# A two-layer hybrid decoder on one core: half-size products in the fourth feed-forward, weight sums on VectorE and by DMA, and memory by stages

## The chip, the core and the metric

The kernel runs on one core of a Trainium2 chip. A core has a matrix engine (TensorE, PE in the rows; its weight loads are listed as PEld), three engines for elementwise work (VectorE or DVE, ScalarE or ACT, GpSimd or POOL), a queue engine (SyncE or SP) and 16 DMA engines that all queues share. The metric is the time of one execution in microseconds (us), lower is better. The time before is the median of three runs.

## The reference, cut to what matters

A sequence of 512 rows with 1024 features goes through two layers. Each layer is a feed-forward, a mixer and a feed-forward. Layer 0 mixes by attention, layer 1 by a state-space scan (S5). So there are four feed-forwards, and the fourth is the last thing computed.

```python
def rmsnorm(x, g):
    xf = x.astype(jnp.float32)
    y = xf * lax.rsqrt(jnp.mean(xf * xf, axis=-1, keepdims=True) + NORM_EPS)
    return (y * g.astype(jnp.float32)).astype(x.dtype)

def swiglu(h, w_gate, w_up, w_down):            # 1024 -> 2816 -> 1024
    return (jax.nn.silu(h @ w_gate) * (h @ w_up)) @ w_down

for i in range(2):
    x = x + 0.5 * swiglu(rmsnorm(x, ffn1_norm[i]), ffn1_gate[i], ffn1_up[i], ffn1_down[i])
    h = rmsnorm(x, mix_norm[i])
    x = x + (diff_fox_mixer(h, ...) if i % 2 == 0 else s5_mixer(h, ...))
    x = x + 0.5 * swiglu(rmsnorm(x, ffn2_norm[i]), ffn2_gate[i], ffn2_up[i], ffn2_down[i])
```

## The kernel before

x lies in on-chip memory, transposed, as 8 tiles of 128 features by 512 rows. Every number that goes into a large product is split into a rounded high part and the rest (`wh` and `wl` for weights, `xh` and `xl` for the normed x, `ah` and `al` for activations), and mm3 (L135) makes a product from three matmuls: high by high, high by low, low by high. Each matmul loads its own 128x128 weight block.

Weights come through the class Stream (L24). A unit is a load on SyncE's queue into one of 4 buffers `raw` of 2048 columns (8 KB in each partition, 1024 KB in all for gate and up). A group is half a unit: ScalarE casts it to `wh` (L77), VectorE subtracts to get `wl` (L79, or L318 and L323 where the subtraction is put off). `ahead` (L101) splits three groups ahead of TensorE and loads three units beyond them.

A feed-forward (ffn, L261) follows ffn_order: 22 tiles of 128 inner features, each one gate and one up product of 8 x 3 matmuls of 512 columns (tile `ps_gu`), and after 6, 12, 17 and 22 tiles a down pass of 8 output blocks (`ps_d`, 6 or 5 tiles each). post (L268) multiplies by the inverse root R, applies silu and splits the activation; upd (L314) adds the block to x. The norm's square sums are collected by norm_sum, stats1 (L221) sums them over partitions on TensorE and takes the root on VectorE in 13 short operations, stats2 (L229) spreads it. In the last down pass the callback `nxt` (in build, L1500) runs for every x block: in feed-forward three it is s5_in (L1215), which copies x into another order (`xp`), stores it to DRAM (dU) and reloads it rearranged (`U`).

Order of the instructions is that of the program text on every engine (`manual_schedule`). Work that fills gaps is written as generators in the list k.bg: attn_setup and s5_tables run beside feed-forward one, s5_ops (L1115) and s5_frames beside two and three. tick (L172) advances them after each gate or up product by 1.4 us of counted VectorE time in feed-forwards two and three (L302) and after each down block but the last pass's by 0.6 of that (L345); a yield of "wait" ends the call early. drain (L183) runs what is left to its end; it stands after feed-forwards one (L1548) and three (L1553).

s5_ops makes the weights of the scan. For each of 4 units it has 4 blocks j: three VectorE operations make `e`, four small matmuls (L1175, tile `ps_s`) follow, then VectorE scales the results, and `dW` and `dY` are stored. At the end of a unit the kernel vector `kq` is stored to DRAM (dK), read back by eight DMAs into `tr`, copied by ScalarE in 16 pieces to `to` (L1209) and stored as `dT`. The scan (s5, L1259) waits for the U tiles, loads dW, dT and dY as `raw`, and uses rotation tables `F5` that s5_frame loads from DRAM, 1 MB for each of four; tables 0 and 1 in the background, 2 and 3 at the first block of the last down pass.

Of the kernel before, what the change touches and what calls it, by code (L numbers as in the profile page):

```python
# [17 lines left out]
GROUPS = [(0, 6), (6, 6), (12, 5), (17, 5)]  # L18
# [5 lines left out]
class Stream:  # L24
# [3 lines left out]
    RAW = 4  # L28

    def __init__(self, nc, raw, hl, ahead_load=3, ahead_split=3):  # L30
        self.nc, self.raw, self.hl = nc, raw, hl
        self.AL, self.AS = ahead_load, ahead_split
        self.units, self.gr = [], []
        self.nl = self.ns = self.cur = self.done = 0
        self.rt, self.wt = {}, {}

    def add(self, ap, ncols, grs, split=True):
        u = len(self.units)
        self.units.append((ap, ncols))
        for a, b in grs:  # L40
            self.gr.append((u, a, b, split))

    def load(self, pieces=((0, 2048),)):
        ap, n = self.units[self.nl]
        t = self.raw.tile([P, 2048], F32, tag="raw", name="raw")
        self.rt[self.nl] = t
        self.nl += 1
        for a, b in pieces:
            self.nc.sync.dma_start(t[:, a:min(b, n)], ap[:, a:min(b, n)])
            yield  # L50

    def load_to(self, u, force=False):
        while self.nl <= min(u, len(self.units) - 1):
            if not force and self.nl - self.RAW >= self.done:
                break
            for _ in self.load():
                pass

    def split_to(self, g, pieces=None, later=None):
        while self.ns <= min(g, len(self.gr) - 1):  # L60
            u, a, b, sp = self.gr[self.ns]
            self.load_to(u, True)
            r = self.rt[u]
            if sp == "pairs":
                h = self.hl.tile([P, 1024], F32R, tag="wh", name="wh")
                z = h[:, :2 * (b - a)].rearrange("p (k two c) -> p k two c", two=2, c=8)
                v = r[:, a:b].rearrange("p (k c) -> p k c", c=8)
                self.nc.scalar.copy(z[:, :, 0], v)
                self.nc.vector.tensor_tensor(z[:, :, 1], v, z[:, :, 0].bitcast(F32), ALU.subtract)
                self.wt[self.ns] = (h, None)  # L70
                self.done = u + 1
            elif sp:
                h = self.hl.tile([P, 1024], F32R, tag="wh", name="wh")
                lo = self.hl.tile([P, 1024], F32R, tag="wl", name="wl")
                for c0, c1 in pieces or ((0, b - a),):
                    rest = (lo[:, c0:c1], r[:, a + c0:a + c1], h[:, c0:c1].bitcast(F32), ALU.subtract)
                    self.nc.scalar.copy(h[:, c0:c1], r[:, a + c0:a + c1])  # L77
                    if later is None:
                        self.nc.vector.tensor_tensor(*rest)  # L79
                    else:  # L80
                        later.append(rest)
                self.wt[self.ns] = (h, lo)
                if self.ns + 1 == len(self.gr) or self.gr[self.ns + 1][0] != u:
                    self.done = u + 1
            else:
                self.wt[self.ns] = (r[:, a:b], None)
            self.ns += 1

    def next(self):
        g = self.cur  # L90
        self.cur += 1
        if g and not self.gr[g - 1][3]:
            self.done = self.gr[g - 1][0] + 1
# [3 lines left out]
    def finish(self):  # L97

        self.done = self.gr[self.cur - 1][0] + 1

    def ahead(self, later=None):  # L101

        g = self.cur
        if g < len(self.gr):
            e = min(g + self.AS, len(self.gr) - 1)
            while not self.gr[e][3] and e > g:
                e -= 1
# [1547 lines left out]
```

## Time and profile before

| | us |
|---|---|
| median of 3 runs | 1898.06 |
| lowest, highest | 1897.71, 1898.67 |
| the profiled execution | 1897.74 |
| its span, first to last instruction | 1895.7 |
| TensorE busy in it | 1881.8 |
| VectorE, ScalarE, GpSimd busy | 1127.4, 671.3, 100.8 |

The four feed-forwards take most of the span: gate, up and down products run from 5 to 376, from 645 to 1383 and from 1531 to 1892 us; attention lies in the first gap, the S5 scan and its gated product in the second. A row of a timeline gives start, duration, engine, line and operation, with the idle time before it and what ended it in square brackets. A row of a group gives the count, the busy time and the mean of one in ns. A row of a table of windows gives the length, then for each engine the busy time and its count of instructions, then the granted clock of TensorE, the busy share of the DMA engines and GB/s.

### The profile page before, as it was taken

Reading aid. Unit: us, or ns where it says so; the run is one execution under the profiler, and the core shown is the slowest. Engines: PE = TensorE matmul, PEld = TensorE weight load, DVE = VectorE, ACT = ScalarE, POOL = GpSimd, SP = SyncE. Lnnn points to the kernel's source line nnn. Section 1 sums busy time; section 2 is a strip of 40 time slices with the busy share of each in tenths; the row PEclk is TensorE's granted clock in tenths of the full one; section 3 lists DMA queues with packets and bytes.
Section 4 is the critical chain, followed back from the end, with each engine's and each line's share of the span. In section 5 each row is a group of like instructions: output and inputs, shape, how many; then the busy total and the mean of one; then the engine's idle time right before and its main releaser. Section 6 shows DMA issues by size and latency. Waiting matters only on the chain.

```text
span 1895.7 us, 22606 instructions
## 1 busy us (share of the span) xinstructions
PE 1881.8 (99%) x8738; PEld 1557.1 (82%) x8740; DVE 1127.4 (59%) x2153; ACT 671.3 (35%) x1104; POOL 100.8 (5%) x184
## 2 busy tenths in 40 slices
PE   8999999999999999999999999999999999999999
PEld 6888888877788888888888888888888888888887
DVE  6787676657685665456557556444484654444443
ACT  5222222434557432322324332322363432222221
POOL 1000111000001000100100100100000000000000
PEclk9999999999999999999999999999999999999999
DMA  6333334234132323423523442433476322323221
GB/s 250 106 106 101 129 107 137 90 111 128 53 85 52 126 80 132 161 100 106 177 102 119 143 145 95 161 128 109 155 247 234 134 86 92 106 84 106 73 100 45
DMA packets 62812, 227.40 MB, mean 120 GB/s; under 512 B 23776, under 2 KB 23904, under 8 KB 46704
## 3 DMA queue, kind: packets, MB, share of 16 engines
q1 hardware_dynamic: 42736, 192.47, 29.7%
q0 software_dynamic: 11504, 31.36, 5.4%
q10 hardware_dynamic: 8464, 2.12, 0.5%
q8 instruction: 69, 1.13, 0.3%
q14 instruction: 39, 0.32, 0.1%
HBM read 196.17 MB, written 26.61 MB: 118 GB/s over the span
## 4 chain that ended last, share of the span: by engine, by line
PE 96%; DVE 1%; ACT 1%; DMA 1%; issue 1%; SPq 0%; DVEq 0%; ACTq 0%
PE ps_gu L137 17%; PE ps_gu L138 17%; PE ps_gu L139 17%; PE ps_d L137 8%; PE ps_d L139 8%; PE ps_d L138 8%; PE ps_p L423 2%; PE ps_p L425 2%; PE ps_p L424 2%; PE ps_g L137 2%; PE ps_g L138 2%; PE ps_g L139 2%; PE ps_s L1175 1%; PE ps_w L137 1%; PE ps_w L138 1%; PE ps_w L139 1%
## 5 line engine op out<-in xcount | busy, mean ns | idle before, releaser
L137 PE MATMUL ps_gu<-xh,wh 128*128 128x512 f32 x1408 | 552.1, 392 | 4.5 <-ACT xh L195 4.3
L138 PE MATMUL ps_gu<-xl,wh 128*128 128x512 f32 x1408 | 548.7, 390 | 0.3 <-DVE xl L196 0.3
L139 PE MATMUL ps_gu<-xh,wl 128*128 128x512 f32 x1408 | 548.8, 390 | 0.0
L77 ACT CAST wh<-raw 128x1024 fp32r<-128x1024 f32 (+3 forms) x354 | 333.9, 947 | 496.9 <-PE ps_d L138 237.3
L79 DVE TENSOR_TENSOR wl<-raw,wh 128x1024 fp32r<-128x1024 f32 (+3 forms) x235 | 260.2, 1110 | 163.9 <-ACT wh L77 162.1
L137 PEld LDWEIGHTS ps_gu<-xh,wh 128*128 128x128 f32 x1408 | 264.6, 188 | 60.6 <-ACT xh L195 4.6
L139 PEld LDWEIGHTS ps_gu<-xh,wl 128*128 128x128 f32 x1408 | 264.6, 188 | 55.7
L138 PEld LDWEIGHTS ps_gu<-xl,wh 128*128 128x128 f32 x1408 | 264.8, 188 | 55.2 <-DVE xl L196 1.2
L137 PE MATMUL ps_d<-ah,wh 128*128 128x512 f32 x704 | 274.9, 391 | 0.0
L139 PE MATMUL ps_d<-ah,wl 128*128 128x512 f32 x704 | 274.0, 389 | 0.0
L138 PE MATMUL ps_d<-al,wh 128*128 128x512 f32 x704 | 273.9, 389 | 0.0
L315 DVE SCALAR_TENSOR_TENSOR x<-ps_d,x 128x512 f32<-128x512 f32 x128 | 88.5, 692 | 183.1 <-PE ps_d L139 182.9
L274 DVE TENSOR_TENSOR u<-ps_gu,R 128x512 f32<-128x512 f32 x88 | 60.8, 691 | 180.7 <-PE ps_gu L139 180.7
L139 PEld LDWEIGHTS ps_d<-ah,wl 128*128 128x128 f32 x704 | 132.2, 188 | 27.7
L138 PEld LDWEIGHTS ps_d<-al,wh 128*128 128x128 f32 x704 | 132.2, 188 | 27.2
L137 PEld LDWEIGHTS ps_d<-ah,wh 128*128 128x128 f32 x704 | 132.2, 188 | 27.1
L277 ACT CAST ah<-u 128x512 fp32r<-128x512 f32 x88 | 54.7, 621 | 253.7 <-DVE u L275 251.3
L272 ACT ACTIVATE g<-g 128x512 f32<-128x512 f32 x88 | 55.6, 632 | 208.2 <-DVE g L271 208.2
L318 DVE TENSOR_TENSOR wl<-raw,wh 128x1024 fp32r<-128x1024 f32 (+2 forms) x101 | 104.8, 1038 | 0.3 <-ACT wh L77 0.3
L279 DVE TENSOR_TENSOR al<-u,ah 128x512 fp32r<-128x512 f32 x88 | 60.9, 692 | 60.5 <-ACT ah L277 60.5
L423 PE MATMUL ps_p<-wh,xh 128*128 128x512 f32 x192 | 78.0, 406 | 0.0
L425 PE MATMUL ps_p<-wh,xl 128*128 128x512 f32 x192 | 75.1, 391 | 0.0
(299 smaller groups left out, 1928.9 us busy)
## 6 DMA issues: line engine op xcount, KB each, us to landing
raw<-in_wgu SPq DMA_DIRECT2D x87, 1024.0 KB, 4.7
raw<-in_wd SPq DMA_DIRECT2D x32, 768.0 KB, 4.3
raw<-in_wd SPq DMA_DIRECT2D x32, 640.0 KB, 3.9
raw<-in_wq SPq DMA_DIRECT2D x12, 1024.0 KB, 4.7
raw<-in_wglu SPq DMA_DIRECT2D x8, 1024.0 KB, 4.8
raw<-in_wo SPq DMA_DIRECT2D x4, 1024.0 KB, 4.8
dW<-t POOLq DMA_DIRECT2D x16, 256.0 KB, 2.3
dY<-y POOLq DMA_DIRECT2D x16, 256.0 KB, 3.5
```

The lines of the kernel that those rows point to most:

```text
L77: self.nc.scalar.copy(h[:, c0:c1], r[:, a + c0:a + c1])
L79: self.nc.vector.tensor_tensor(*rest)
L137: nc.tensor.matmul(ps, wh, xh, start=start, stop=False)
L138: nc.tensor.matmul(ps, wh, xl, start=False, stop=False)
L139: nc.tensor.matmul(ps, wl, xh, start=False, stop=stop)
L272: S.activation(g1, g1, AF.Silu)
L274: V.tensor_tensor(u1, up, k.R, ALU.mult)
L279: V.tensor_tensor(al, u1, ah.bitcast(F32), ALU.subtract)
L315: V.scalar_tensor_tensor(k.x[:, d], p, 0.5, k.x[:, d], ALU.mult, ALU.add)
L318: V.tensor_tensor(*a)
L423: T.matmul(ps[t], xh, w[:, c], start=kk == 0, stop=False)
L425: T.matmul(ps[t], xl, w[:, c], start=False, stop=kk == 7)
```

## The change

The first three feed-forwards keep their products, in another order: gate and up of a tile are made together from two units of 1024 columns, first the even input blocks, then the odd ones; down passes are spread between them, in groups of 4 tiles and a last one of 6. All units are of 1024 columns (512 KB), with 8 `raw` buffers.

The fourth feed-forward takes tiles in 11 pairs. Of the 2 x 2 x 2 block products (halves of the pair, even and odd input blocks, halves of the rows) it makes seven products P1 to P7 of half size and combines them: x enters as sums of blocks (`form_*`), made at the end of the S5 stage, and the weights as sums of blocks. Each product is 24 matmuls of 256 columns. The block of P5 is used three times (P5, P6, P3), each time with another block added. For the first four pairs VectorE adds blocks that are loaded anyway; for the others GpSimd's queue issues a DMA that accumulates from DRAM into the buffer. The first sums of P5 and P7 are made by such a DMA in every pair.

In the background, the part of s5_tables that makes the rotation tables becomes s5_rotate and runs in feed-forward two, ahead of s5_ops. s5_ops gets more waits. Stores on GpSimd's queue are put off by two ticks (class Later). All four tables are loaded by s5_in. drain after feed-forward three moves into its last down pass, before the first update of x, by the callback `leave`; units marked `late` (dW, dT, dY) are loaded only when k.bg is empty.

Memory is given out by stages (`region`): the general pool shrinks from 36 to 29 tiles, and tiles for x, the scan and the forms share the rest in turn.

```diff
-GROUPS = [(0, 6), (6, 6), (12, 5), (17, 5)]
+NPAIR = 11
+GROUPS = [(0, 2), (2, 2), (4, 2), (6, 2), (8, 3)]
...
-    RAW = 4
+    RAW = 8
...
+        if isinstance(ap, tuple):
+            self.nc.vector.tensor_tensor(t[:, :n], *[self.rt[u][:, :n] for u in ap], ALU.add)
...
+        if more is not None:
+            self.accs.append((self.clock + 2, self.nl - 1, more))
+
+    def flush(self, u=-1):
+
+        now = [a for a in self.accs if a[0] <= self.clock or a[1] <= u]
...
+            self.nc.gpsimd.dma_start(self.rt[v][:, :self.units[v][1]], ap, accum_op=ALU.add)
+
+    def fill(self, upto=None, force=False):
+
+        n = len(self.units) if upto is None else upto + 1
+        while self.nl < n:
+            ap, _, _, late = self.units[self.nl]
+            if not force and (self.live >= self.RAW or isinstance(ap, tuple) or late and not self.ready()):
                 break
...
+SLOT = {"P1": 0, "P2": 1, "P5": 3, "P6": 4, "P3": 2, "P7": 5, "P4": 6}
...
+    o = [("first", 0), ("P6", 0), ("P1", 1), ("P3", 0)]
+    downs = [("d", (g, q)) for g in range(len(GROUPS) - 1) for q in range(4)]
+    for j in range(1, NPAIR):
+        a, b = ([downs.pop(0)], [downs.pop(0)]) if j > 2 else ([], [])
+        o += [("P5", j), ("P7", j - 1)] + a + [("P2", j), ("P6", j), ("P4", j - 1)] + b
+        o += (j < NPAIR - 1) * [("P1", j + 1)] + [("P3", j)]
+    return o + [("P7", NPAIR - 1), ("d0", 0), ("P4", NPAIR - 1), ("last", 0)]
...
+        elif kind == "P5":
+            st.entry(unit("P5", j), then=unit("P1", j) if j < 4 else wgu[j, 0])
+        elif kind == "P6":
+            st.entry(unit("P5", j), then=unit("P2", j) if j < 4 else wgu[j, 1])
+        elif kind == "P3":
+            st.entry(unit("P5", j))
...
+    def prod(ps, wl, s, start, kps=range(4)):
+        w, lo = wl
+        for kp in kps:
+            for h in range(2):
+                c = slice(h * 512 + kp * 128, h * 512 + kp * 128 + 128)
+                o, xh, xl = ps[:, h * 256:h * 256 + 256], k.Fh[:, s, kp], k.Fl[:, s, kp]
+                first = start and kp == 0 and h == 0
+                for i, (a, b) in enumerate(((w, xh), (w, xl), (lo, xh))):
+                    nc.tensor.matmul(o, a[:, c], b, start=first and i == 0, stop=kp == 3 and i == 2,
+                                     skip_group_check=True)
...
+    def last():
+        t = tiles(len(GROUPS) - 1)
+        for d in (1, 2):
+            begin(d, 5)
+            slot(n=3 - d)
+        blk(*held[0], 4 * 128, t[4], False, False)
+        slot(n=1)
+        if leave:
+            leave()
+        for d in range(8):
+            if d < 3:
+                p, w, lo = held[d]
+                blk(p, w, lo, 5 * 128, t[5], False, True)
+            else:
+                begin(d, 6)
+                p = held[d][0]
+            later = []
+            if d >= 2:
+                slot(later)
+            upd(d, p)
...
+            nxt(d)
...
+            if (j, i, l) == (0, 0, 0) and sums:
+                run_out(sums)
+            elif (j, i, l) == (0, 0, 1):
+                stats1(k)
+            elif (j, i, l) == (0, 1, 0):
+                stats2(k)
...
+        if (kind, j) == ("P6", 0):
+            stats1(k)
+        if (kind, j) == ("P1", 1):
+            stats2(k)
+        slot()
+        tick(k, rate)
...
             yield
             tt(e[:, :512], e[:, :512], t[:, :512], ALU.add)
             yield "wait"
+            yield "wait"
...
-        Q.dma_start(kk[:, 0:8, :], kq[:, :256])
-        Q.dma_start(kk[:, 8:16, :], k.zz)
-        yield "wait"
+        Q.store(kk[:, 0:8, :], kq[:, :256])
+        for _ in range(4):
+            yield "wait"
...
-        k.U5 = []
-        s5_frame(k, 2)
-        s5_frame(k, 3)
+        k.U5, k.F5 = [], {}
+    if d % 2 == 0:
+        s5_frame(k, d // 2)
...
-NGEN = 36
+NGEN = 29
...
-            ffn(k, nt(1), 2.0, sums)
+            k.bg += [attn_setup(k, I["rel"], I["aux"]), s5_tables(k, I["s5par"])]
+            ffn(k, nt(1), 2.0, sums, plain=True)
             drain(k)
-            attn(k, nt(2))
-            k.bg += [s5_ops(k, I["s5par"], I["s5bc"]), s5_frames(k)]
-            ffn(k, nt(3), 1.4)
-            ffn(k, lambda d: s5_in(k, d), 1.4)
-            drain(k)
-            s5(k, nt(5))
+            attn(k, nt(2), lambda: None, I["aux"])
+            k.bg += [s5_rotate(k), s5_ops(k, I["s5par"], I["s5bc"])]
+            ffn(k, nt(3), 1.4, plain=True)
+            ffn(k, lambda d: s5_in(k, d), 1.4, plain=True,
+                leave=lambda: (drain(k), k.region(big=2, hls=1, gen2=8)))
+            s5(k, ft(5), lambda: k.region(pad=112, form=1))
             ffn(k, lambda d: nc.sync.dma_start(out[:, d], k.x[:, d]))
```

## Rows read from the trace of the kernel before

**Rows 1.** The page: busy times of the engines, and the chain's shares by engine.
```profile
PE 1881.8 (99%) x8738; PEld 1557.1 (82%) x8740; DVE 1127.4 (59%) x2153; ACT 671.3 (35%) x1104; POOL 100.8 (5%) x184
...
PE 96%; DVE 1%; ACT 1%; DMA 1%; issue 1%; SPq 0%; DVEq 0%; ACTq 0%
```
**Rows 2.** Windows: length; PE, PEld, DVE, ACT, POOL busy; clock, DMA share, GB/s.
```profile
1560.00:1600.00 40.00, 40.00 (x178) 33.10 (x178) 18.39 (x23) 11.15 (x15) 0.00 (x0) 1.00 0.26 86
```
**Rows 3.** Windows of the start.
```profile
8.00:12.00 4.00, 1.00 (x2) 0.50 (x3) 1.99 (x3) 2.85 (x5) 0.00 (x0) 0.85 1.05 376
16.00:24.00 8.00, 8.00 (x37) 6.64 (x36) 7.25 (x11) 7.26 (x11) 0.00 (x0) 1.00 1.01 426
```
**Rows 4.** Timeline of VectorE and ScalarE after the third feed-forward: start, duration, operation.
```profile
1383.34 0.69 DVE L315 SCALAR_TENSOR_TENSOR x<-ps_d,x 128x512 f32<-128x512 f32 x1 [0.97 <-PE ps_d L139]
1384.60 1.12 ACT L1224 COPY xp<-x 128x512 f32<-128x512 f32 x1
...
1395.87 0.69 DVE L1276 TENSOR_TENSOR U<-U,rs_y 128x512 f32<-128x512 f32 x1 [0.68 <-DMA U<-dU]
```
**Rows 5.** Windows around the start of the scan.
```profile
1385.00:1395.00 10.00, 10.00 (x69) 7.35 (x67) 8.34 (x22) 3.05 (x4) 0.00 (x0) 1.00 0.97 264
1395.00:1405.00 10.00, 10.00 (x92) 10.00 (x91) 9.32 (x21) 6.56 (x13) 0.00 (x0) 1.00 0.96 334
```
**Rows 6.** Timeline of TensorE in the scan and in attention.
```profile
1391.95 5.47 PE L1284 MATMUL ps_S<-U,raw 128*128 128x64 f32 x48
...
567.85 0.28 PE L782 MATMUL ps_s<-fb 68*128 68x256 f32 x1
567.98 0.60 PE L648 MATMUL ps_t<-cst,e 128*128 128x128 f32 x4
...
572.15 0.40 PE L782 MATMUL ps_s<-fb 68*128 68x512 f32 x1
572.39 0.40 PE L137 MATMUL ps_w<-oh,wh 128*128 128x512 f32 x1
```
**Rows 7.** Timeline of VectorE at the fourth feed-forward's root, first of 13 and next.
```profile
1543.31 0.16 DVE L147 TENSOR_SCALAR rs_m<-ps_st 128x4 f32<-128x4 f32 x1 [4.08 <-PE ps_st L225]
...
1545.57 1.23 DVE L79 TENSOR_TENSOR wl<-raw,wh 128x1024 fp32r<-128x1024 f32 x1
```
**Rows 8.** Groups by line and shape: count, busy us, mean ns, idle before.
```profile
L79 DVE TENSOR_TENSOR wl<-raw,wh 128x1024 fp32r<-128x1024 f32 x159 | 193.9, 1223 | 103.8 <-ACT wh L77 102.8
L127 DVE TENSOR_TENSOR t<-ps_s,s5par 128x256 f32<-128x256 f32 x32 | 13.4, 419 | 0.0
L127 DVE TENSOR_TENSOR kq<-ps_s,kq 128x32 f32<-128x32 f32 x32 | 5.8, 182 | 0.0
...
L77 ACT CAST wh<-raw 128x1024 fp32r<-128x1024 f32 x222 | 232.1, 1049 | 329.1 <-PE ps_d L138 156.2 <-PE ps_gu L138 135.7 <-PE ps_p L425 14.6
L77 ACT CAST wh<-raw 128x768 fp32r<-128x768 f32 x65 | 54.2, 834 | 98.3 <-PE ps_d L138 53.0 <-PE ps_gu L138 34.0 <-issue 5.1
L195 ACT ACTIVATE xh<-x,cst 128x512 fp32r<-128x512 f32 x40 | 28.3, 721 | 53.2 <-DVE x L315 21.6 <-DVE x L1384 17.9 <-DVE x L838 11.8
L206 ACT ACTIVATE sq<-x 128x512 f32<-128x512 f32 x42 | 25.5, 619 | 3.5 <-DVE x L315 3.5
```
**Rows 9.** DMA issues: count, KB each, median us from issue to landing.
```profile
raw<-in_wgu SPq DMA_DIRECT2D x87, 1024.0 KB, 4.7
raw<-in_wd SPq DMA_DIRECT2D x32, 640.0 KB, 3.9
...
tr<-dK POOLq DMA_DIRECT2D x32, 128.0 KB, 2.9
```
**Rows 10.** Line 1209: ns (least, median, most), first and last start in us.
```profile
L1209 ACT COPY to<-tr x64: 322/326/338, 784.5 to 1232.4; 128x128 f32<-128x128 f32 x64
```
**Rows 11.** Timeline of GpSimd's queue at the tail of the last unit.
```profile
1204.64 0.56 POOL L1197 DMA_DIRECT2D dK<-kq  x1 [8.00 <-DVE kq L127]
...
1208.20 4.19 POOL L1202 DMA_DIRECT2D tr<-dK  x8 [2.46 <-DMA dK<-zz]
```

More of the change, by code (lines that the diff above doesn't have):

```diff
@@ L70, in split_to @@
                 self.wt[self.ns] = (h, None)
-                self.done = u + 1
+                self.unref(u)
             elif sp:
[L73 to L77, printed above, removed]
+                h = hl.tile([P, 1024], F32R, tag="wh", name="wh")
@@ L97, in finish, with ahead @@
     def finish(self):
[L99 to L107, printed above, removed]
-            if self.gr[e][3]:
-                self.split_to(e, later=later)
-            self.load_to(self.gr[e][0] + self.AL)
+        for u in self.open:
+            self.unref(u)
+        self.open = []
+    def ahead(self, later=None, n=None):
+        e = min(self.cur + (self.AS if n is None else n), len(self.ents) - 1)
+        while e >= self.cur and not (self.ents[e][1] and self.ents[e][3] is None):
+            e -= 1
+        if e >= self.ns:
+            self.split_to(e, later=later)
+        self.clock += 1
+        self.flush()
+        self.fill()
 class Counted:
@@ L128, in __getattr__, with __init__, store, flush @@
         return call
+class Later:
+    def __init__(self, q):
+        self.q, self.n, self.todo = q, 0, []
+    def store(self, *a):
+        self.todo.append((self.n + 2, a))
+    def flush(self, all=True):
+        while self.todo and (all or self.todo[0][0] <= self.n):
+            self.q.dma_start(*self.todo.pop(0)[1])
+    def tick(self):
+        self.n += 1
+        self.flush(False)
+    def dma_start(self, *a):
+        self.flush()
+        self.q.dma_start(*a)
 class Kern:
@@ L172, in tick @@
 def tick(k, us):
+    k.late.tick()
     end = k.cv.us + us
@@ L199, in norm_sum, with squares @@
+def squares(k):
+    k.sq = [k.G("sq")[:, :512] for _ in range(8)]
+    for d in range(8):
+        k.nc.scalar.activation(k.sq[d], k.x[:, d], AF.Square)
 def norm_sum(k, d):
@@ L252, in ffn_units, with plain_plan, plain_units @@
+def plain_plan():
+    o = []
+    downs = [("d", (g, q)) for g in range(len(GROUPS) - 1) for q in range(4)]
+    for j in range(NPAIR):
+        for i in range(2):
+            o.append(("gu", (j, i)))
+            if j > 1 and downs:
+                o.append(downs.pop(0))
+    return o + [("d0", 0), ("last", 0)]
+def plain_units(st, wgu, wd4, wd6):
+    for kind, j in plain_plan():
         if kind == "gu":
[L253 to L258 removed]
@@ new lines, in ffn @@
+    for kind, j in plain_plan() if plain else ffn_plan():
+        if kind == "gu":
+            gu_tile(*j)
+            continue
+        elif kind == "first":
+            first()
+        elif kind == "d0":
+            begin(0, 4)
+        elif kind == "last":
+            last()
+            continue
+        elif kind == "d":
+            down(*j)
+            continue
+        else:
+            step(kind, j)
+        if (kind, j) == ("P6", 0):
+            stats1(k)
+        if (kind, j) == ("P1", 1):
+            stats2(k)
+        slot()
+        tick(k, rate)
@@ L380, in attn_setup @@
     V.tensor_tensor(rlo, rb[:32, :4], rh.bitcast(F32), ALU.subtract)
-    yield "wait"
+    for _ in range(3):
+        yield "wait"
     for h in range(4):
@@ L1168, in s5_ops @@
             tt(e[:, :512], e[:, :512], t[:, :512], ALU.add)
+            yield "wait"
             yield "wait"
```

691 lines of the change are left out of this document (455 added, 236 removed).

## The prediction

> **What bounds the kernel now.** I read the page's busy times and chain first: TensorE is busy for 99% of the span and holds 96% of the chain that ended last [rows 1]. So time is won only by fewer or shorter matmuls, and a stall of TensorE's queue costs its full length. Next came the busy times of a stretch inside the fourth feed-forward [rows 2]: 178 matmuls touch a window of 40 us, some two of them cut off by its edges, so a 128x512 matmul takes 40/176.5 = 0.227 us from start to start. (A listed duration, 0.4 us, is a pipelined one and adds up to nothing.) VectorE is busy there for 18 of 40 us, ScalarE for 11, the DMA engines for a quarter. Then I looked for places where TensorE is not the limit: the first 16 us [rows 3], and the 12 us between the third feed-forward's last block and the S5 scan [rows 4, 5].
>
> All sums go against the profiled execution: 1897.74 us (span 1895.73 and 2.0 around it), 0.3 us below the median of three.
>
> **Gate and up of the fourth feed-forward: -29.8.** Before: 22 tiles x 2 x 24 = 1056 matmuls of 512 columns, 1056 x 0.227 = 239.5 us. After: 11 pairs x 7 products x 24 = 1848 matmuls of 256 columns. No row has a run of those, so I bound one. Each needs a fresh 128x128 weight block: 48 matmuls of 64 columns, each with its own block, take 5.47 us [rows 6], so weights can follow each other every 0.114 us or faster. The matmul of line 782 is followed by the next start after 0.13 us at 256 columns and 0.24 us at 512 [rows 6]; both hold a hand-over to another kind of matmul, and the difference, 0.11 us, is 256 columns alone. I take half of 0.227, 0.1135 us, which lies between; the ends are 0.11 and 0.13. 1848 x 0.1135 = 209.7: a gain of 29.8 us (36 at 0.11, nothing at 0.13).
> The Trainium skill ("TensorE: Matmul & The Clock Gate", Back-to-back issue gap) gives 262 cycles for 256 columns, an estimated 0.109 us, and warns that weight loads and matmuls set the spacing together; by it the gain would be some 38 us. Its figure for 512 columns, about 216 ns, is below this trace's 227, so the row decides.
>
> **New stalls in the same stage: +3.** The norm's inverse root takes 13 short VectorE operations from 1543.31 to 1545.6 us, 2.3 us [rows 7]. stats2 now follows stats1 by one product of 24 x 0.1135 = 2.7 us instead of 5.4, and VectorE's queue also has a weight subtraction of 1.22 us [rows 8] and an eviction; TensorE will wait about 2.5 us. The first down product wants pair 1 four slots after its last product: 0.5 us. VectorE's cover is thin: a pair has 7 subtractions (8.5 us), 2 weight sums (2.4), and 9 operations of 0.69 and one of 1.22 for gating (7.4), 18.3 us in 7 x 2.72 = 19.0, until downs start with pair 3; from there 23.5 in 29.9. It holds because three blocks are split ahead; without that the first three pairs lose whatever VectorE is over. The 36 accumulating DMAs (GpSimd's queue, 512 KB) have no like in this trace. Landing rises from 3.9 us at 640 KB to 4.7 at 1024 KB [rows 9], so 512 KB is an estimated 3.6 us, 4.7 if the destination's bytes count too; the block is split next four products later (13.6 us with a down), so I take nothing.
>
> **The background that no longer fits: +28.** This term decides. s5_rotate and s5_ops are advanced by tick; a call stops at a yield "wait" or when its allowance of VectorE time is used up. Walking the calls of the kernel before through feed-forwards two and three, s5_ops needs 112 of the 136 and ends at 1233 us; the trace's last `to` copy starts at 1232.4 [rows 10], so the walk can be trusted. After: 77 calls in each feed-forward (44 at 1.4 us, 32 at 1.12, one at 1.4), 154 in all. s5_rotate, moved here from the first one (60 us by the counter), takes 37. s5_ops takes 4 waits, then for each of 4 units 4 blocks of five to six calls (a wait more than before) and 12 waits of tail: about 144. Together 181, so 27 are missing: block j=2, block j=3 and the tail of the last unit are left, and `leave` drains them at once, ahead of the last eight down blocks.
> I follow that from T0, the moment TensorE comes to it. Without a stall the last x would be written 2.0 + 5 x 4.08 + 0.9 = 23.3 us later, which is 1384.0 in this trace [rows 4]; T0 stands for 1360.7. VectorE has done j=2's operands by then. Before j=3's matmuls it has 2 x 0.42 + 2 x 0.18 [rows 8] and five of 0.69 us, 4.7 us for which TensorE stands still; eight more end at T0 + 9. Then the kernel vector goes through DRAM: 3.6 us from the store's issue to the first read's, 4.2 for eight reads [rows 11], and the last lands 2.4 us after [rows 9], T0 + 19. ScalarE must finish 16 copies of 0.33 us [rows 10] before anything later in its queue: T0 + 23.5. Then two squares (0.62) [rows 8] and copies of x (1.12) [rows 4], and the cast of down block 5 (0.83) [rows 8]: T0 + 28. TensorE ran out of split blocks at T0 + 16 and idles 12 us. Three blocks later the last x is there, at T0 + 43, 19.7 us late.
> Behind it SyncE's queue is held up: its eight stores of x start with ScalarE's first copy (T0 + 25), and before the last reload come 2 MB of stores, 2 MB of reloads, 3 of the 4 MB of rotation tables (all four now load here, two did before) and 4 MB of dW blocks, which wait until the background is empty. 11 MB at the 264 to 334 GB/s of this region [rows 5] are 33 to 42 us, so the last reload lands at T0 + 60 to 69. In the trace VectorE took it up at 1395.87, after 0.68 us of waiting [rows 4]: T0 + 35. That is 25 to 34 us late; I take 28, nearer the faster rate, as the blocks come in long rows. The ends are 18 (the copies alone, nothing queued) and 36.
>
> **Start: +1.** Between 8 and 12 us TensorE is busy 1.0 us of 4 [rows 3]: its weights and x are queued with 2 MB of x. Loading the even x blocks first may win up to 6 us. But stats1 now stands after the second product, not the third, and ScalarE's eight gains, five casts and eight squares (0.72, 1.05 and 0.62 us) [rows 8] reach it about 5 us late. From -4 to +4.
>
> **The rest: +1.** Feed-forwards one to three keep their matmuls; eight more updates of 0.69 us each lie in VectorE's idle half [rows 2]. s5_rotate's 32 table stores move with it, on GpSimd's queue, which is busy for 5% [rows 1]. Seven fewer general tiles and 512 KB blocks in eight buffers may add waits for a free buffer, which no row shows: 0 to 4, taken as 0, since loads run five blocks ahead. The form tiles at the end of S5 add about 3 us after the last x, covered by 60 matmuls (6.8 us) that need even blocks only; without that cover they cost 3. After a long idle TensorE's granted clock may fall to the lower of its levels (1.2 of 2.4 GHz), as at the start (a mean of 0.85 of full [rows 3]): 1 us.
>
> Sum: 1897.7 - 29.8 + 3 + 28 + 1 + 1 = 1900.9.
>
> **The rivals.** *The remainder is cheap* (faster): if the trip through DRAM is short enough, or the drained copies early enough, that ScalarE is back before TensorE has used its split blocks, only the 2 MB more of tables stays in SyncE's queue (6 us at 310 GB/s): 1900.9 - 28 + 6 = 1879, from 1870 to 1889. For it: the trip's parts are single cases or medians. Against: the copies stand ahead of the casts in ScalarE's queue in any case. *No gain from half size* (slower): if a 256-column matmul takes the 0.13 us of its row, the gain is nil and the kernel 1931; it decides from 239.5/1848 = 0.1296 us. Against: the weights' pace of 0.114. *Accumulating DMAs are late* (slower): a pair's block is used three times, 13.6 us apart. Past that, each of 14 accumulations (pairs 4 to 10) holds up ScalarE's casts for the excess: at 15 us, 20 us in all, 1921. *Short loads* (slower): if 512 KB loads land one behind the other, 55 + 36 + 16 of an estimated 3.6 us and 8 smaller ones make 410 us in a stage of 330: 1980. Against: 426 GB/s with several 1 MB loads in flight [rows 3].
> The Trainium skill ("DMA: Bandwidth & Descriptors", Bandwidth) has the rule behind that last one: batch DMAs to at least 1 MiB. The 426 GB/s of loads in flight together speak for overlap.
>
> **How the numbers follow.** Forecast 0.52 (its own range 1890 to 1912), cheap remainder 0.30, no gain 0.07, late accumulations 0.08, short loads 0.03. The 8-in-10 range takes in most of the cheap case and half of the late one: 1875 to 1922. A measurement of this kernel can tell about 0.2% (3.8 us) from no change. Faster: 0.29 of the cheap case and 0.11 of the forecast's lower end, 0.40. Same: 0.17, nearly all the forecast. Slower: 0.25 of it and the three slow rivals, 0.43.
>
> **What would show it.** Gate and up: starts 0.113 us apart, the fourth feed-forward near 333 us. The drain: matmuls of the S5 blocks and 16 `to` copies right ahead of the third feed-forward's last down blocks, TensorE gaps of about 5 and 12 us there, and the last reload of U some 60 us after the first of those matmuls. Wrong would be: no gap there (the calls were miscounted), a pace near 0.13, or ScalarE waiting for accumulations.

## The result

The changed kernel takes 1927.3 us (median of four runs, 1925.8 to 1928.4) against 1897.9 us of the kernel before: a ratio of 1.015, 95% interval 1.0132 to 1.0169. It is slower. The forecast was 1901 with a range of 1875 to 1922, so the time lies 5 us above the range. The profiled execution has a span of 1924.0 us, 28.3 us more than before [rows 1].

The page of the changed kernel, busy times of the engines (engine, busy us, share of the span, instructions):

```profile
PE 1883.0 (98%) x9532; PEld 1594.7 (83%) x9532; DVE 1214.0 (63%) x2239; ACT 722.0 (38%) x1147; POOL 133.6 (7%) x220
```

TensorE is as busy as before (1881.8 us) although the fourth feed-forward has fewer columns to do. Busy time alone says no more than that. I therefore cut the span at five points that both traces have: the first product of attention, the last down product of the third feed-forward, the moment VectorE takes up the last reload of U, the last product of the S5 stage's gate, and the end. Each row is the time between two of them, in us; the kernels of the later columns come from the experiments below. Differences in the text are taken before rounding.

| stretch | before | after | e2_rate3 | e11_best | e14_keep2 |
|---|---|---|---|---|---|
| start to attention | 375.9 | 384.4 | 384.6 | 374.1 | 372.9 |
| attention, second and third feed-forward | 1007.1 | 1027.9 | 1007.0 | 1006.8 | 1006.9 |
| last down product to last reload of U | 13.0 | 23.5 | 21.1 | 16.2 | 16.5 |
| from there to the end of the S5 stage | 135.3 | 141.2 | 141.1 | 140.9 | 130.7 |
| fourth feed-forward | 364.5 | 346.9 | 346.8 | 346.9 | 348.4 |
| span | 1895.7 | 1924.0 | 1900.6 | 1885.0 | 1875.4 |

After minus before: +8.6, +20.8, +10.6, +5.9, -17.6, together +28.3. The stage that was changed for its own sake did become shorter. The four other stretches became longer.

TensorE's waits in the changed kernel (for whom; total us, times, longest):

```profile
PE ps_d L211 <- ACT wh L118: 8.0, 1, 8.0
PE ps_s L1577 <- DVE e L178: 7.9, 2, 4.0
PE ps_st L386 <- DVE acc L178: 5.7, 1, 5.7
PE ps_y L1744 <- DVE m L1734: 3.5, 1, 3.5
PE ps_d L211 <- ACT ah L532: 2.0, 1, 2.0
...
PE ps_f L516 <- DVE g L562: 1.7, 1, 1.7
PE ps_f L516 <- ACT P L521: 1.7, 1, 1.7
```

The first two lines are the drain, the later one first: S5's matmuls wait twice for VectorE, then the down products wait for a cast that stands behind the `to` copies in ScalarE's queue. The third and fifth are in the first feed-forward, the fourth in the S5 stage, the last two in the fourth feed-forward. TensorE's timeline at the drain (start, duration, operation, idle time before it; eight rows of L1577 are one block j, since the trace lists 128 of them for 16 blocks), and the granted clock in the middle of it:

```profile
1365.95 1.14 PE L1577 MATMUL ps_s<-s5ic,e 128*128 128x144 f32 x8
1371.05 2.26 PE L1577 MATMUL ps_s<-s5ic,e 128*128 128x144 f32 x8 [3.96 <-DVE e L178]
1377.27 2.26 PE L1577 MATMUL ps_s<-s5ic,e 128*128 128x144 f32 x8 [3.96 <-DVE e L178]
...
1398.64 0.80 PE L211 MATMUL ps_d<-ah,wh 128*128 128x512 f32 x1 [7.98 <-ACT wh L118]
```

```profile
1375.00:1380.00 5.00, 2.73 (x10) 2.66 (x11) 3.65 (x9) 0.00 (x0) 0.54 (x1) 0.50 0.27 105
```

The clock was at half (1.2 of 2.4 GHz) from 1371 to 1381 and again from 1395 to 1402 us: eight S5 rows took 2.26 us behind the first wait and 1.14 before it. The three waits make 15.9 of the second row's 20.8 us. The slow matmuls between and behind them account for the rest: against the full-clock pace of the same matmuls they took an estimated 5 us more.

ScalarE in the same place, the copies and what they hold up:

```profile
1388.36 0.33 ACT L1610 COPY to<-tr 128x128 f32<-128x128 f32 x1 [15.77 <-DMA tr<-dK]
...
1391.74 3.04 ACT L1610 COPY to<-tr 128x128 f32<-128x128 f32 x13 [0.96 <-DMA tr<-dK]
...
1397.77 1.56 ACT L118 CAST wh<-raw 128x768 fp32r<-128x768 f32 x2
```

ScalarE waited 15.8 us for the trip through DRAM, copied sixteen tiles, and reached the cast at 1397.8, 31.8 us after the drain began at 1365.95 (the prediction: 28 us with the cast done).

VectorE taking up the reloads of U, and the fourth feed-forward's half-size products:

```profile
1430.87 0.69 DVE L1672 TENSOR_TENSOR U<-U,rs_y 128x512 f32<-128x512 f32 x1 [6.44 <-DMA U<-dU]
...
1435.84 0.69 DVE L1672 TENSOR_TENSOR U<-U,rs_y 128x512 f32<-128x512 f32 x1 [1.50 <-DMA U<-dU]
```

```profile
1599.72 0.28 PE L516 MATMUL ps_f<-Fh,wh 128*128 128x256 f32 x1
1599.84 0.28 PE L516 MATMUL ps_f<-Fl,wh 128*128 128x256 f32 x1
...
1601.96 0.28 PE L516 MATMUL ps_f<-Fl,wh 128*128 128x256 f32 x1
```

Nineteen matmuls start from the first of these up to the last: 2.24/19 = 0.1179 us for a matmul of 256 columns. The forecast took 0.1135.

The clock in the S5 stage, in the changed kernel and then in the kernel before (length; busy us of PE, PEld, DVE, ACT, POOL; granted clock, DMA share, GB/s):

```profile
1422.00:1432.00 10.00, 8.76 (x79) 8.62 (x78) 2.15 (x4) 5.76 (x10) 0.00 (x0) 1.00 1.00 319
1432.00:1472.00 40.00, 36.45 (x174) 36.21 (x173) 27.50 (x54) 15.71 (x27) 0.00 (x0) 0.51 0.61 201
1472.00:1482.00 10.00, 10.00 (x40) 7.67 (x40) 8.03 (x14) 4.29 (x7) 0.00 (x0) 0.76 0.84 272
```

```profile
1417.00:1431.00 14.00, 14.00 (x59) 13.09 (x59) 11.78 (x25) 8.80 (x16) 0.00 (x0) 0.51 0.77 241
```

The granted clock is at its lower level for some 45 us, against 14 before.

### The profile page after: what moved, and what is told of

Read it like the earlier page. It is cut to its first block, busy times and chain, and to the rows that moved or that the text cites. A ratio compares the mean times of both kernels' runs of the same rounds, so it can differ in the third digit from the quotient of the medians.

```text
span 1924.0 us, 24894 instructions
## 1 busy us (share of the span) xinstructions
PE 1883.0 (98%) x9532; PEld 1594.7 (83%) x9532; DVE 1214.0 (63%) x2239; ACT 722.0 (38%) x1147; POOL 133.6 (7%) x220
## 5 line engine op out<-in xcount | busy, mean ns | idle before, releaser
L118 ACT CAST wh<-raw 128x1024 fp32r<-128x1024 f32 (+2 forms) x356 | 362.4, 1023 | 642.7 <-issue 208.1
L211 PE MATMUL ps_gu<-xh,wh 128*128 128x512 f32 x1056 | 414.8, 393 | 1.5 <-ACT xh L271 1.5
L212 PE MATMUL ps_gu<-xl,wh 128*128 128x512 f32 x1056 | 411.8, 390 | 0.3 <-DVE xl L272 0.3
L213 PE MATMUL ps_gu<-xh,wl 128*128 128x512 f32 x1056 | 411.9, 390 | 0.0
L121 DVE TENSOR_TENSOR wl<-raw,wh 128x1024 fp32r<-128x1024 f32 (+2 forms) x265 | 314.6, 1191 | 128.4 <-ACT wh L118 124.4
L516 PE MATMUL ps_f<-Fh,wh 128*128 128x256 f32 x616 | 173.5, 282 | 3.5 <-DVE g L562 1.7
L516 PE MATMUL ps_f<-Fl,wh 128*128 128x256 f32 x616 | 173.2, 281 | 0.0
L516 PE MATMUL ps_f<-Fh,wl 128*128 128x256 f32 x616 | 173.1, 281 | 0.0
L213 PEld LDWEIGHTS ps_d<-ah,wl 128*128 128x128 f32 x704 | 133.0, 189 | 28.3 <-DVE wl L123 0.5
L516 PEld LDWEIGHTS ps_f<-Fh,wh 128*128 128x128 f32 x616 | 116.3, 189 | 4.8 <-DVE g L562 2.2
L516 PEld LDWEIGHTS ps_f<-Fh,wl 128*128 128x128 f32 x616 | 117.6, 191 | 0.0
```

The costliest lines, as they stand in the source:

```text
L118: S.copy(h[:, c0:c1], r[:, c0:c1])
L121: V.tensor_tensor(*a)
L211: nc.tensor.matmul(ps, wh, xh, start=start, stop=False)
L212: nc.tensor.matmul(ps, wh, xl, start=False, stop=False)
L213: nc.tensor.matmul(ps, wl, xh, start=False, stop=stop)
L516: nc.tensor.matmul(o, a[:, c], b, start=first and i == 0, stop=kp == 3 and i == 2, skip_group_check=True)
```

## The experiments

My theory after the result: the background that no longer fits (the drain) costs the third feed-forward its 20.8 us, and through the late reload of U and the idle time also most of the next two rows, so that taking the drain away gives back some 41 us.

**e1_rotate_first** undoes the one move that made the background too long:

```diff
-            k.bg += [attn_setup(k, I["rel"], I["aux"]), s5_tables(k, I["s5par"])]
+            k.bg += [attn_setup(k, I["rel"], I["aux"]), s5_tables(k, I["s5par"]), s5_rotate(k)]
-            k.bg += [s5_rotate(k), s5_ops(k, I["s5par"], I["s5bc"])]
+            k.bg += [s5_ops(k, I["s5par"], I["s5bc"])]
```

> s5_rotate goes back behind s5_tables into the first feed-forward; the rest is the changed kernel. Theory (the background did not fit: 27 of 181 calls were left and drained ahead of the third feed-forward's last eight down blocks): s5_ops alone needs 144 of 154 calls, so no S5 block is left. The two TensorE gaps of 3.96 us and the one of 7.98 us go, the last reload of U comes 35 us after the point where the drain stood (it was 70), and the lower clock of the S5 stage shrinks from 45 us to some 14: 1927.3 - 34.8 - 5.9 = 1886.6. If the 2 MB more of rotation tables still hold SyncE's queue, 6 us of that stay: 1893. Rival (the stage is late because of the new order of the stream, 512 KB blocks and changed memory regions): the gaps stay, 1927.

Measured: 1903.7 us (ratio to before 1.0034, interval 1.0021 to 1.0047). **e2_rate3** leaves the order and gives each call more of VectorE:

```diff
-            ffn(k, nt(3), 1.4, plain=True)
+            ffn(k, nt(3), 3.0, plain=True)
-            ffn(k, lambda d: s5_in(k, d), 1.4, plain=True,
+            ffn(k, lambda d: s5_in(k, d), 3.0, plain=True,
```

> The allowance of VectorE time per call goes from 1.4 to 3.0 us in the second and third feed-forward; s5_rotate stays in the second. Theory (calls were too few): walked by the same counter the background ends at call 138 of 154, so the drain is empty: 1886.6 as in the other, to 1893 with the tables' bytes. Rival (VectorE's time is short, not the calls): bursts of three operations push the gating operations back, TensorE waits in the second and third feed-forward, and part of the gain goes: 1895 to 1927.

Measured: 1903.9 us (1.0034, 1.002 to 1.0048). Two different ways to make the background fit give the same time, and TensorE's three waits at the drain are gone in both. So the drain is shown as the cause, and it is worth 23.5 us, not 41. The second row of the table is back at 1007.0 (1007.5 in e1_rotate_first). The third and fourth are not (22.8 and 141.5 there). What TensorE waits for now, and the last reload of U, in e2_rate3:

```profile
PE ps_y L1744 <- DVE m L1734: 6.6, 1, 6.6
PE ps_st L386 <- DVE acc L178: 4.1, 1, 4.1
PE ps_d L211 <- ACT ah L532: 2.0, 1, 2.0
```

```profile
1412.69 0.69 DVE L1672 TENSOR_TENSOR U<-U,rs_y 128x512 f32<-128x512 f32 x1 [1.48 <-DMA U<-dU]
```

U's last reload comes 21.1 us after the last down product, with nothing drained; the kernel before needed 13.0. My theory fell for these two rows: they have a cause of their own.

**e3_queue_only** keeps the allowance of 3.0 and holds the S5 weight blocks back to the point of the drain:

```diff
-        st.ready = lambda: not k.bg
+        k.gone = []
+        st.ready = lambda: bool(k.gone)
-                leave=lambda: (drain(k), k.region(big=2, hls=1, gen2=8)))
+                leave=lambda: (drain(k), k.gone.append(1), k.region(big=2, hls=1, gen2=8)))
```

> Allowance 3.0 us as in the run before, so that nothing is drained, but the S5 weight blocks and all loads behind them are still held back to the point of the drain. It tells the two parts of the delay apart. Queue theory (SyncE's bytes set the last reload of U): 12 MB from that point at 264 to 334 GB/s are 38 to 48 us, so U lands 3 to 13 us later than without the hold: 1890 to 1900. If the queue alone made the 34.8 us, 1920. If the drained copies and matmuls alone made them, 1887, as without the hold.

Measured: 1903.6 us, U's last reload 20.3 us after the last down product: no difference. This run tells less than I wanted. In e2_rate3 the first of these blocks is loaded at 1363.3 us, just ahead of that point, with no hold at all, since the eight load buffers are in use until then. So the hold moved one block of 512 KB, from 1363.3 to 1375.5, and tells next to nothing of the queue under the drain.

**e9_frames_first**, on e2_rate3, loads the four rotation tables ahead of the first store of x:

```diff
         k.U5, k.F5 = [], {}
-    if d % 2 == 0:
-        s5_frame(k, d // 2)
+        for q in range(4):
+            s5_frame(k, q)
```

> On the kernel with allowance 3.0 (1903.9): all four rotation tables are loaded at the point where the drain stood, ahead of the first store of x, instead of two by two between the stores. Without the drain U's last reload is still some 8 us late, counted from the last down product (21.1 against 13.0), and the S5 stage from there 6 us longer. Theory (SyncE's queue is bound by bytes from 1374 us on while the DMA engines idle from 1365 to 1375): 2 to 2.7 MB move into the idle time, U's last reload comes 6 to 8 us sooner, and with it some of the 6 us: 1891 to 1898. Rival (the stores and reloads wait for ScalarE's copies, not for bytes): U's last reload stays at 21 us, 1904. Rival for the 6 us (the lower clock there has its own cause): they stay, 1897.

Measured: 1898.6 us (0.9998, 0.9985 to 1.0011), 5.3 us less than e2_rate3. The DMA engines of e2_rate3, in the ten microseconds ahead of the stores and in the stores' 35 us, and then those of this run (columns as above):

```profile
1365.00:1375.00 10.00, 10.00 (x46) 8.29 (x45) 2.67 (x4) 3.99 (x6) 0.00 (x0) 1.00 0.47 172
1375.00:1410.00 35.00, 35.00 (x209) 28.25 (x207) 20.95 (x37) 22.45 (x30) 0.00 (x0) 1.00 0.97 301
```

```profile
1365.00:1375.00 10.00, 10.00 (x46) 8.29 (x45) 2.69 (x5) 4.09 (x6) 0.00 (x0) 1.00 0.96 323
1375.00:1410.00 35.00, 35.00 (x209) 28.29 (x207) 24.02 (x44) 22.32 (x29) 0.00 (x0) 1.00 0.92 290
```

The idle half of the first window is filled (share 0.47 to 0.96, some 1.5 MB more), and U's last reload comes 16.1 us after the last down product instead of 21.1. So 5.0 of the 8.1 us by which U was late in e2_rate3 came from the place of the tables in the queue. The S5 stage behind it hardly moved, as its rival said (139.3 from 141.1).

**e8_start**, on e2_rate3, treats the first row of the table: stats1 one product later in the first feed-forward, and a smaller allowance for the tables there.

```diff
-            elif (j, i, l) == (0, 0, 1):
+            elif (j, i, l) == ((0, 1, 0) if sums else (0, 0, 1)):
                 stats1(k)
-            elif (j, i, l) == (0, 1, 0):
+            elif (j, i, l) == ((0, 1, 1) if sums else (0, 1, 0)):
                 stats2(k)
-            if wait and l == 0:
+            if wait and l == (1 if sums and (j, i) == (0, 1) else 0):
                 post()
-            ffn(k, nt(1), 2.0, sums, plain=True)
+            ffn(k, nt(1), 1.4, sums, plain=True)
```

> On the kernel with allowance 3.0 (1903.9): in the first feed-forward stats1 stands after the third product instead of the second, stats2 after the fourth, and the allowance of the tables there goes from 2.0 to 1.4 us. The changed kernel reaches attention 8.6 us later than before: some 4.3 us at the start, with a TensorE gap of 5.7 us ahead of stats1, and some 4.3 us near 210 us, with a gap of 2.0 us behind tables that fill VectorE, both followed by matmuls at half clock. Theory (these two places are the loss): both gaps go, attention starts at 376 to 378 us, 1894 to 1896. Rival for the first (the third product's weights are not there, since loads fill the DMA engines until 28 us): the gap moves by one product, 1899. Rival for the second (it is the order of the gating operations, not VectorE's load): the gap at 210 us stays, 1899.

Measured: 1891.0 us (0.9962, 0.9949 to 0.9976), 12.9 us less than e2_rate3. Attention starts at 374.0 us, 10.7 us sooner, and both waits are gone. The place of the second one, in the changed kernel and then in this run:

```profile
150.00:200.00 50.00, 50.00 (x223) 41.39 (x222) 45.08 (x144) 12.73 (x15) 0.00 (x0) 1.00 0.24 85
200.00:210.00 10.00, 8.50 (x38) 6.71 (x36) 9.36 (x25) 0.79 (x2) 0.00 (x0) 1.00 0.28 87
210.00:220.00 10.00, 9.49 (x34) 7.45 (x35) 9.30 (x21) 3.53 (x5) 2.23 (x4) 0.83 0.60 203
```

```profile
150.00:200.00 50.00, 50.00 (x222) 41.40 (x221) 41.76 (x122) 13.04 (x16) 0.00 (x0) 1.00 0.28 95
200.00:210.00 10.00, 10.00 (x46) 8.29 (x45) 9.02 (x27) 2.09 (x3) 0.00 (x0) 1.00 0.31 105
210.00:220.00 10.00, 10.00 (x46) 8.29 (x45) 8.16 (x24) 3.19 (x4) 0.00 (x0) 1.00 0.30 105
```

VectorE was busy 45 of 50 us, some 27 of them with the tables (35 in all in the same stretch of the kernel before), and then the down products waited for an activation behind them. The two edits were not run apart, but the traces tell the two places apart: the first down product starts at 66.7 us instead of 73.2, so 6.6 of the 10.7 us are won at the start and 4.1 behind it, at the second place.

**e4_plain4** makes the fourth feed-forward, drain and all, of full-size products:

```diff
-        ffn_units(st, I["wgu"][3], I["wd4"][3], I["wd6"][3], False)
+        F(3)
-            s5(k, ft(5), lambda: k.region(pad=112, form=1))
-            ffn(k, lambda d: nc.sync.dma_start(out[:, d], k.x[:, d]))
+            s5(k, nt(5), lambda: k.region(big=2))
+            ffn(k, lambda d: nc.sync.dma_start(out[:, d], k.x[:, d]), plain=True)
```

> The fourth feed-forward is made of full-size products like the three others; all else is the changed kernel, drain included. Theory (the half-size products save 217.7 against 239.5 us, less 4 us of new stalls): the stage goes back to 364 us, 1927.3 + 17.6 = 1945. Rival (the loaded blocks, accumulations and forms give the gain back elsewhere, in the S5 stage too): 1927 to 1935.

Measured: 1944.0 us (1.0249, 1.0233 to 1.0266), 16.7 above the changed kernel. The half-size products are worth 17 us, and they take nothing back in the S5 stage (140.4 us from the last reload of U to its end, with full-size products behind it, against 141.2).

**e10_n128** asks what sets their pace:

```diff
-                    nc.tensor.matmul(o, a[:, c], b, start=first and i == 0, stop=kp == 3 and i == 2,
+                    m = 256 if kp + i == 0 else 128
+                    nc.tensor.matmul(o[:, :m], a[:, c], b[:, :m], start=first and i == 0, stop=kp == 3 and i == 2,
```

> What sets the pace of a half-size product: 22 of the 24 matmuls of each work on 128 of their 256 columns (the other columns are left out, so the activations are wrong), all else is the changed kernel. Measured were 0.2267 us at 512 columns and 0.1178 at 256. Theory (a pace by columns with a fixed part, 0.1089 us for 256 columns and 0.009 fixed): the spacing at 128 columns is 0.063 us, the 1848 matmuls shrink to about half and the stage to what VectorE's work allows. Rival (each fresh block of weights takes 0.1178 us, and the columns are hidden): the spacing stays at 0.118 us, and the time at 1927.

Measured: 1966 us in a single run, 39 us slower with almost half of the gate and up columns left out. At the full clock:

```profile
1709.85 0.28 PE L517 MATMUL ps_f<-Fh,wh 128*128 128x128 f32 x1
...
1711.74 0.27 PE L517 MATMUL ps_f<-Fh,wl 128*128 128x128 f32 x1
...
1711.86 0.33 PE L517 MATMUL ps_f<-Fh,wh 128*128 128x256 f32 x1
```

Seventeen matmuls start from the first of these lines up to the second, in 1.899 us by the trace: 0.112 us each, the same as the 64-column matmuls with a fresh weight block [rows 6], whose starts lie 0.112 us apart. So with a fresh block the pace did not fall below 0.112 us at either width. Both expectations miss: the pace is not by columns down to 0.063, and it is not 0.118 at every width. At 256 columns, 0.118 is a little above this pace and a little above half of 0.227 (0.1135); what adds the rest, no run shows. And the slowdown is the clock:

```profile
1580.00:1590.00 10.00, 7.98 (x69) 7.70 (x68) 8.06 (x11) 6.58 (x9) 0.86 (x1) 0.98 0.46 106
...
1600.00:1640.00 40.00, 40.00 (x190) 40.00 (x189) 19.46 (x20) 15.18 (x19) 1.71 (x2) 0.50 0.38 106
1640.00:1680.00 40.00, 40.00 (x189) 40.00 (x190) 18.14 (x20) 11.92 (x15) 1.72 (x2) 0.50 0.38 105
...
1700.00:1720.00 20.00, 20.00 (x156) 19.04 (x156) 13.66 (x16) 9.39 (x12) 3.47 (x4) 1.00 0.78 193
```

From 1590 to 1688 TensorE ran narrow matmuls without a pause at half clock (0.213 us each). The clock was back at full at 1692, behind the first 512-column down products, which start at 1688.4. The fall at 1589.7 followed a wait of 1.8 us at 1589 (for a tile `ps_f` that ScalarE has to empty). The changed kernel has the same wait, and its matmuls of 256 columns went on at the full clock:

```profile
1587.77 0.38 PE L516 MATMUL ps_f<-Fh,wh 128*128 128x256 f32 x1 [1.73 <-ACT P L521]
```

```profile
1590.00:1610.00 20.00, 20.00 (x173) 20.00 (x173) 16.77 (x29) 11.33 (x15) 1.71 (x2) 1.00 0.62 176
```

In e14_keep2 (below) the clock did fall at this wait, but came back after 3.4 us of 256-column matmuls. So the wait alone does not make 100 us; that the narrow matmuls held the clock down is the likely reading, and was not tried apart.

**e11_best** puts e2_rate3, e8_start and e9_frames_first together.

> All edits together on the changed kernel: allowance 3.0 us in the second and third feed-forward, 1.4 in the first, stats1 after the third product there, and the four rotation tables loaded first. If the gains add: 1903.9 - 9 - 10 = 1885. If only the start's part holds: 1895; if only the tables' part: 1894; if neither: 1904.

Measured: 1886.6 us (0.9932, 0.9919 to 0.9944). The gains add to within 2 us. The S5 stage is still 5.6 us longer than before, and its clock is at half from 1407 to 1437.

**e12_keep** fills TensorE's wait for the scan with dummies (matmuls of 512 columns whose result nobody reads, 0.216 us each), on e11_best; **e14_keep2** fills the next wait too:

```diff
     frame(1)
+    keep_busy(k, 12)
     fY(0)
     scan(1)
+    keep_busy(k, 12)
     fY(1)
```

> On the kernel with all edits together (1886.6): twelve more dummy matmuls of 512 columns (2.6 us) stand ahead of the first S5 output product, where TensorE waits 2.2 us for the scan. In that kernel the granted clock falls to half behind this wait, at 1407, and comes back at 1437; before it fell at 1417 and came back at 1431. The stage of the output products takes 29 us instead of 20. Theory (the idle 2.2 us bring the clock down): without the idle time it stays up or falls later, 4 to 8 us are won: 1879 to 1883. Rival (the 64-column matmuls themselves bring it down, with or without a gap): nothing is won, 1886 to 1887.

> On the run with twelve dummy matmuls ahead of the first output product (1882.6): twelve more ahead of the second one, where TensorE now waits 2.3 us, and the granted clock falls to half 4 us later, at 1416, until 1431. Theory (idle time brings the clock down): with no idle time left between the scan's products it stays at full, and the stage is 4 to 6 us shorter: 1877 to 1880. Rival (the 64-column matmuls bring it down whatever is idle): the clock falls at the same place and the dummies cost what they fill, 1882 to 1885.

Measured: 1882.6 us (0.9915, 0.99 to 0.993) with the first, 1877.8 us (0.9889, 0.9868 to 0.9909) with both. The granted clock over the same stage in e11_best, in e12_keep and in e14_keep2:

```profile
1407.00:1437.00 30.00, 30.00 (x135) 29.23 (x135) 20.93 (x39) 14.12 (x25) 0.00 (x0) 0.50 0.56 180
```

```profile
1417.00:1431.00 14.00, 14.00 (x64) 13.84 (x65) 8.45 (x20) 7.28 (x13) 0.00 (x0) 0.50 0.68 203
```

```profile
1404.00:1434.00 30.00, 29.19 (x208) 24.70 (x206) 26.03 (x50) 18.79 (x33) 0.00 (x0) 1.00 0.70 222
```

With one wait filled the clock falls at the next one; with both filled it does not fall in this stage, and 5.2 us of useless work wins 8.8 us. The kernel before had the same loss in a smaller measure (14 us at half clock). The dummies fill the idle time and are 512 columns wide: which of the two keeps the clock up, these runs do not tell apart. The fourth feed-forward of e14_keep2 is 1.5 us longer, with the 3.4 us at half clock named above.

**e13_acc_all**, on e11_best, makes the weight sums of the first pairs by accumulating loads as well:

```diff
-            st.entry(unit("P5", j), then=unit("P1", j) if j < 4 else wgu[j, 0])
+            st.entry(unit("P5", j), then=unit("P1", j) if j < 0 else wgu[j, 0])
-            st.entry(unit("P5", j), then=unit("P2", j) if j < 4 else wgu[j, 1])
+            st.entry(unit("P5", j), then=unit("P2", j) if j < 0 else wgu[j, 1])
```

> On the kernel with all edits together (1886.6): the weight sums of the first four pairs, too, are made by accumulating loads, but for the very first (7 of 8 sums go from VectorE to DMA). Theory (neither way is on the path: the accumulated block lands 7 us after the issue and is split 13 us after): no change, 1886 to 1887. Rival (the accumulations are late where loads are dense): ScalarE's casts wait and TensorE with them, some 2 us for each, up to 1900. Rival (VectorE's sums hold up the gating of the first pairs, which causes the wait of 1.7 us there): 1885.

Measured: 1893.7 us (0.9976, 0.9965 to 0.9988), 7.1 us slower than e11_best. A new wait of TensorE ends at 1595 us, followed by matmuls at half clock until 1598.6. ScalarE's casts ahead of it wait twice for a load, 8.8 us until 1582.4 and 1.6 until 1591.4, and both times it is an accumulating one that lands 0.1 us before:

```profile
PE ps_f L516 <- ACT ah L532: 5.5, 1, 5.5
```

```profile
1591.44 1.99 ACT L118 CAST wh<-raw 128x1024 fp32r<-128x1024 f32 x2 [1.56 <-DMA raw<-in_wgu]
```

So for the first pairs VectorE's sums do earn their place: there the accumulating loads come late. My theory (neither way is on the path) fell for these pairs.

## Why the prediction was wrong, step by step

**Gate and up, -29.8: the pace was mis-sized.** 1848 x 0.1179 = 217.9 us against 239.5 is -21.6. The bounds, 0.11 and 0.13, held it. The choice inside them failed: half of the 512-column pace assumes that all of it shrinks with the columns, and with 128 columns the pace is still 0.112. The row that I had set aside as a bound, the weights at 0.114, would have done little better (-28.8): 256 columns take longer than either neighbour, and why stays open. The Trainium skill ("TensorE: Matmul & The Clock Gate", Back-to-back issue gap) gave an estimated 0.109 for 256 columns; the measured 0.118 is above it. Its warning that weight loads and matmuls set the spacing together fits e10_n128, where half of the columns gone takes only 0.006 us off a matmul.

**New stalls of the same stage, +3: the size was right, by luck.** Two waits of 1.7 us, and -17.6 + 21.6 = +4.0 in all. But neither is where I put it. One, at 1587.8, is for a tile that ScalarE empties late, behind three casts; the other, at 1887.3, is for VectorE in the last pair. The waits for the root and for the first down product did not come. VectorE's thin cover held between the two.

**The background, +28: the mechanism was right, the size nearly, the split wrong.** That calls were missing is shown: with enough allowance, or with s5_rotate moved back, the drain is gone, and no other edit was needed for that. No run counts them, but 27 fits: less the 12 of the tail they are 15 calls, and a block takes five to six, so a third block had to be left beside the two that I wrote. The trace shows three. That is the second gap of 3.96 us, with which ScalarE reached its cast at T0 + 31.8, where I had it done at T0 + 28, and VectorE took up the last reload at T0 + 70, where I had it land at T0 + 60 to 69. The drain costs 20.8 us in the row that holds it, where I had 19.7; that the two are so near is partly luck, since I had 16.7 us of waits (4.7 and 12, measured 15.9) and nothing for the clock that fell behind them. Of the 8 us more that I gave to the loads behind it, the measured 10.6 are mostly there without any drain (8.1 in e2_rate3): I made one chain of two causes. That also spoils the rival "the remainder is cheap": it kept 6 us for the tables, the place was right and the size near, but its 1879 was out of reach, since e2_rate3, with no remainder at all, takes 1903.9.

**Start, +1 with 4 either way: +8.6.** The late stats1 was seen, and its wait is there (5.7 us). By TensorE's waits for x (the kernel before, then the changed one) the even blocks first won 2.8 us, not up to 6:

```profile
PE ps_gu L137 <- ACT xh L195: 4.3, 1, 4.3
```

```profile
PE ps_gu L211 <- ACT xh L271: 1.5, 1, 1.5
```

The second loss, around 210 us, was missing (4.1 us by e8_start): I read VectorE's idle half from a stretch of the fourth feed-forward [rows 2] and used it for the first, where the tables bring VectorE to 45 us of 50.

**The rest, +1: +5.9.** I gave the clock 1 us after a long idle. It was at half for 45 us in the S5 stage, against 14 before. In e11_best it fell at the wait for the scan, and filling the waits took the fall away; that the wait for the late U set it off in the changed kernel, at 1432.5, is argued from the same pattern and was not tried. I had read the clock at the start only [rows 3] and not in the stage that the delay would hit.

The cut at the last reload of U hides how much this is. TensorE itself starts the scan 9.0 us after the last down product in the kernel before, in the changed one and in e2_rate3 alike, so a late reload reaches it only through the waits behind that start. From the last down product to the end of the S5 stage, both rows together, in us:

| | before | after | e2_rate3 | e9_frames_first | e11_best | e14_keep2 |
|---|---|---|---|---|---|---|
| length | 148.3 | 164.8 | 162.1 | 155.4 | 157.2 | 147.1 |
| at half clock | 14 | 44 | 34 | 27 | 31 | 0 |
| TensorE's waits for U and the scan | 1.5 | 4.7 | 6.6 | 2.0 | 2.2 | 0.4 |

An estimate from these rows, the added waits and half of the added time at half clock, is 18, 15, 7 and 9 us above the kernel before for the first four of the others; measured are 16.5, 13.8, 7.1 and 8.9. So by this estimate the greater part of the changed kernel's 16.5 us in these two rows is time at half clock, for which my sum had 1 us.

**The other rivals.** Short loads land after 3.5 us and TensorE stands still for none. The rule of the Trainium skill ("DMA: Bandwidth & Descriptors", Bandwidth), batches of at least 1 MiB, did not decide here. The accumulating loads of the changed kernel land after 7.0 us, twice as late, and no cast of the fourth feed-forward waits for one; e13_acc_all shows where they do.

```profile
raw<-in_wgu SPq DMA_DIRECT2D x186, 512.0 KB, 3.5
...
raw<-in_wgu POOLq DMA_DIRECT2D x36, 512.0 KB, 7.0
```

By the terms of the sum, the misses all have one sign: 8.2 + 1.0 in the fourth feed-forward, 7.6 at the start, 3.4 at the drain and behind it, 4.9 in the S5 stage, together 25 us, which is the span's +28.3 less the forecast's +3.2. So no single term failed: the pace of the half-size products was mis-sized, and the wait behind the tables and the half clock of the S5 stage were put at next to nothing.

## What to carry to other kernels

A change that fills a stage's slots also takes away the slots that background work used: count its calls against the slots that are left, and give them more per call before anything is drained ahead of a queue that others need. Read the load of an engine, and the clock, from the very stage that a step touches, not from a quieter one. Where narrow matmuls wait for another engine, dummies in the wait can be worth more than they cost: here 1886.6 became 1877.8. With its background fitted in alone, the changed kernel is still 0.3% slower than the kernel before; with all edits of e14_keep2 it is 1.1% faster.

## What the runs showed of the hardware

A matmul of the gate and up products with a fresh 128x128 weight block starts every 0.112 us at 128 columns, 0.118 at 256 and 0.227 at 512, all at the full clock: below 256 columns next to nothing is won. At half clock, 128 columns take 0.213 us each. After a wait of 1.8 us a stream of 128-column matmuls without a pause ran at half clock for 100 us, so less work took 39 us longer; the clock came back when 512-column matmuls followed. In the S5 stage the clock fell at waits of 2.2 and 2.3 us beside 64-column matmuls, and did not fall with both filled.
